# Attention products of 256 columns as three one-pass products, with split operands, rotary scores per pair of heads, and the first and last pair's steps moved

## The chip, the cores and the metric

The kernel runs on one core of a Trainium2 chip. The metric is the device time of one execution in microseconds. Three runs of the kernel before gave 2061.98, 2063.13 and 2064.1 us, a median of 2063.13 us.

## The reference

A decoder trunk of two layers over 256 positions, width 2048, all in float32. Layer A is chunked spatial gating (12 groups of 128 channels), layer B is multi-head latent attention (12 heads), and both stand beside a cross-attention of 4 heads of 128 channels into 256 memory tokens. After each follows a gated FFN of width 5632. What the change touches is the attention of layer B and the memory attention of both layers:

```
# MLA (layer B), per head h and block of 128 queries
q = (rmsnorm(q_lat, g_q_lat) @ w_uq).reshape(B, S, 12, 128 + 64)
q_nope, q_rope = q[..., :128], apply_rope(q[..., 128:], cos, sin)
s = (q_nope . (c_kv @ w_uk) + q_rope . k_rope) * 192 ** -0.5      # causal
o = softmax(s) @ (c_kv @ w_uv)

# memory attention, per layer, 4 heads of 128
s = einsum('bshd,bmhd->bhsm', q, k) * 128 ** -0.5
o = einsum('bhsm,bmhd->bshd', softmax(s), v)

x = x + concatenate([main, memory], -1) @ w_out
```

`rmsnorm`, the projections `w_in`, `w_kv_a`, `w_mem_kv`, the gMLP gate and the FFN are the rest, and the change leaves them alone but for the buffers that they pass through.

## The kernel before, in words

**Weights.** Every weight matrix is streamed in chunks of 128 x 1024 float32: SyncE (SP) starts the DMA into `raw` (4 buffers, line 100 on), ScalarE (ACT) rounds it to a `whi` tile of the one-pass type fp32r (L113, or L109 for the head-wise chunks of `w_uq`), and VectorE (DVE) writes the rest, raw minus whi, to `wlo` (L114, L110). `split_tile` (L94) gives both 5 buffers. A tile is written anew only when TensorE (PE) has read the chunk five earlier.

**Products.** Activations are held in the same form, a high half and a low half beside each other (`xhl`, `qhl`, `chl`, `mainhl`). A float32 product is then three one-pass products: whi x high (L152), whi x low (L153) and wlo x high (L155), 256 columns each. `gemm_tm` (L184 to L186) does the same with the activations as the stationary side and 512 columns.

**The heads' products** are different: their operands are plain float32 tiles, and PE works a float32 product itself, shown as two records each. These are, with `P` = 128: memory scores (L584, `kT` by `qm`, two products per head), memory output (L619, `mv` by `pT`, two per head), MLA scores without rotary part (L956, 128 columns for the first block of queries and 256 for the second), MLA rotary part (L957, `qr` by `krz`, the same sizes, each head by itself), and attention output (L990 with 256 columns, L991 with 128). PE also transposes the softmaxed scores (`turn` L981, `mturn` L608), and ACT copies the result from PSUM to `pT` (L983, L612).

**Layer B's loop** goes over the six pairs of heads, i = 0 to 5. One pass holds: `queries(i)` (two chunks of `w_uq`, ACT copies the result to `qn`), `rotary(i)` (`rotate` on GpSimd, POOL: L865, four L868, L869), `keys(i)` (one chunk of `w_uk`), for the pair before last the `turn`s and the memory `mturn`, for the last pair `scores` with softmax (DVE L963 to L974, ACT L969), then `attend` and `mout` for the pair before last, and `mscores(i-1)` (DVE L590 to L600, ACT L595). Ahead of the loop `values(0..2)` project `c_kv` through `w_uv` into `v`, which lies with the name `scratch` in the memory of the layer's first operand. Behind the loop stand `scores` of the last pair, and the last two pairs' `turn` and `attend` are hooks among the chunks of `w_out` (chunks 0, 1 and 3).

**Order.** The program is written once, and a scheduler decides, by its own estimate of times, in which order each engine gets its instructions; each engine then works its own list strictly in order, waiting on semaphores. So a written move shows as other neighbours in these lists.

Of the kernel before, what the change touches and what calls it, by code (L numbers as in the profile page):

```python
# [69 lines left out]
class Kernel:  # L70
# [359 lines left out]
    def start(self):  # L430
        nc, t, tc = self.nc, self.t, self.tc
        self.x = self.ap.tile([P, NB, S], F32, name="xT")
        self.xhl = self.ap.tile([P, NB, 512], F32R, tag="xhl", name=self.uid("xhl"))
# [5 lines left out]
        with tc.tile_pool(name="st", bufs=1) as st:  # L439
# [12 lines left out]
            def put_x(k, acc):  # L452
                for i in range(2):
                    self.split_gain(self.xhl[:, k + i, :], acc[:, i * S : (i + 1) * S], self.gain("g_mix", k + i))
                nc.scalar.activation(self.x[:, k : k + 2, :], acc.rearrange("p (k s) -> p k s", k=2), AF.Copy)
# [124 lines left out]
    def memory_scores(self, l, h, q, pool):  # L580
        nc = self.nc
        acc = self.psum()
        for sb in range(2):
            nc.tensor.matmul(  # L584
                acc[:, sb * S : (sb + 1) * S], q[:, sb * P : (sb + 1) * P], self.kT[l][:, h, :], start=True, stop=True
            )
        scale = 128 ** -0.5
        a3 = acc.rearrange("p (a m) -> p a m", a=2)
        mx = self.tmp(pool, [P, 2], "mx", 4)
# [3 lines left out]
        den = self.tmp(pool, [P, 2], "den", 4)  # L593
# [9 lines left out]
    def memory_turn(self, p, pool, bufs=2):  # L603
# [11 lines left out]
    def memory_out(self, l, h, pT, hl):  # L615
        nc, v = self.nc, self.mv[l]
        o = self.psum()
        for mb in range(2):
            nc.tensor.matmul(o[:, :S], v[:, mb, h * P : (h + 1) * P], pT[:, mb * S : (mb + 1) * S], start=mb == 0, stop=mb == 1)  # L619
        self.split(hl[:, GH + h, :], o[:, :S])  # L620
# [5 lines left out]

    def new_hl(self):
        self.xhl = self.ap.tile([P, NB, 512], F32R, tag="xhl", name=self.uid("xhl"))
        self.ssum = self.tmp(self.cp, [P, S], "ssum", 2)

    def next_operand(self, j, gain):
        x = self.x[:, j, :]
        if gain is None:
            self.split(self.xhl[:, j, :], x)
        else:
            self.split_gain(self.xhl[:, j, :], x, gain)
# [20 lines left out]
    def ffn(self, l, after=None, to_tokens=None, tokens=None):  # L657
# [5 lines left out]
        with self.tc.tile_pool(name=self.uid("ff"), bufs=1) as fp:  # L663
            g0 = 0
            for part, ng in enumerate(FF_GROUPS):
# [11 lines left out]
                for g in range(g0, g0 + ng):  # L677
# [14 lines left out]
                    self.gemm_fm(self.rows(up, g * 512, 512), ks, 4, lambda k: xhl[:, k, :], eg, hooks=first if g == 0 else {})  # L692
                    self.gemm_fm(self.rows(up, FF + g * 512, 512), ks, 4, lambda k: xhl[:, k, :], ev, hooks=turns)
# [21 lines left out]
    def layer_a(self):  # L715
        nc, t, tc = self.nc, self.t, self.tc
        w, xhl, rt, rb = t["w_in_a"][0], self.xhl, self.rt, self.rb
        x = lambda k: xhl[:, k, :]
        ks = list(range(NB))
        with ExitStack() as ctx:  # L720
# [5 lines left out]
            wT = la.tile([P, GH, P], F32, name="wT")  # L726
            bb = la.tile([P, GH, P], F32, name="bb")
# [52 lines left out]
            p = {}  # L780

            def scores(h):
                p[h] = self.memory_scores(0, h, qm[:, h, :], la)
# [4 lines left out]
            for c in range(3):  # L788
# [11 lines left out]
                if c < 2:  # L800
                    h = 2 * c
                    hooks = {
                        0: [lambda: gates(9)] if c == 0 else [],
                        2: [lambda h=h: scores(h)],
                        3: [lambda h=h: scores(h + 1)],
                        5: [lambda h=h: turn(h), lambda h=h: turn(h + 1)],
                        6: [lambda h=h: self.memory_out(0, h, p[h], hl)],
                        7: [lambda h=h: self.memory_out(0, h + 1, p[h + 1], hl)],
# [5 lines left out]
    def layer_b(self):  # L814
# [7 lines left out]
        x = lambda k: xhl[:, k, :]  # L822
        mm, tt = nc.tensor.matmul, nc.vector.tensor_tensor
        with tc.tile_pool(name="lb", bufs=1) as lb:
# [4 lines left out]
            krz = lb.tile([P, 2, S], F32, name="krz")  # L829
            nc.gpsimd.memset(krz, 0.0)  # L830
            qm = lb.tile([P, MH, S], F32, name="qm1")
            lt = ctx.enter_context(tc.tile_pool(name="lt", bufs=1))

# [28 lines left out]
            def rotate(dst, a):  # L862
# [6 lines left out]
                nc.gpsimd.tensor_tensor(dst, m, n, ALU.subtract)  # L869
# [14 lines left out]
            def rotate_key():  # L884
# [7 lines left out]
                for j in range(2):  # L892
                    r = slice(j * ROPE, (j + 1) * ROPE)
                    nc.gpsimd.tensor_tensor(krz[r, j, :], m[r, :], n[r, :], ALU.add)
# [8 lines left out]
            scratch = self.ap.tile([P, NB * 512], F32, tag="xhl", name="scratch")  # L903
            v = scratch[:, : 2 * GW].rearrange("p (a c) -> p a c", a=2)
            wuv = t["w_uv"][0].rearrange("r h v -> r (h v)")

            def values(c):
                def ev(tb, acc):
                    nc.scalar.activation(v[:, tb, c * 512 : (c + 1) * 512], acc, AF.Copy)
# [3 lines left out]
            for c in range(3):  # L913
                values(c)
            ctx.close()
            lp = ctx.enter_context(tc.tile_pool(name="lp", bufs=1))
# [6 lines left out]
            def queries(pr):  # L923
# [9 lines left out]
                qn[pr] = self.tmp(lp, [P, 3, S], "qn", 2)  # L933
# [3 lines left out]
            def keys(pr):  # L937
                kn[pr] = self.tmp(lp, [P, 2, S], "kn", 2)
# [6 lines left out]
            def rotary(pr):  # L945
                qr[pr] = self.tmp(lp, [P, S], "qr", 2)
                rotate(qr[pr], qn[pr][:, 2, :])

            def scores(h):
                pr, j = divmod(h, 2)  # L950
                sc = self.psum()
                for qb in range(2):
                    n = P * (qb + 1)
                    o = sc[:, qb * P : qb * P + n]
                    q = slice(qb * P, (qb + 1) * P)
                    mm(o, qn[pr][:, j, q], kn[pr][:, j, :n], start=True, stop=False)  # L956
                    mm(o, qr[pr][:, q], krz[:, j, :n], start=False, stop=True)  # L957
                mx = self.tmp(lp, [P, 2], "mx", 4)
                den = self.tmp(lp, [P, 2], "den", 4)
                p = self.tmp(lp, [P, 3 * P], "p", 3)  # L960
                part = (slice(0, P), slice(P, 3 * P))
                for qb in range(2):
                    nc.vector.tensor_tensor_reduce(  # L963
                        out=p[:, part[qb]], in0=sc[:, part[qb]], in1=self.mask[:, (1 - qb) * P :], scale=1.0, scalar=-3.0e38,
# [12 lines left out]
            def turn(h):  # L977
# [4 lines left out]
                pT = self.tmp(lp, [P, 512], "pT", 3)  # L982
                nc.scalar.activation(pT[:, : 3 * P], acc[:, : 3 * P], AF.Copy)  # L983
                pa[h] = pT

            def attend(h):
                pT = pa.pop(h)
# [149 lines left out]
```

## Time and profile before

| | |
|---|---|
| runs, median | 2063.13 us |
| profiled execution | 2063.35 us, of which span 2061.6 us (1.75 us lie around the span) |
| granted TensorE clock | 0.999 |
| PE | 2051.8 us busy, 16316 products |
| DVE | 1375.7 us busy (67%) |
| ACT | 1075.2 us busy (52%) |
| POOL | 141.0 us busy (7%) |
| HBM traffic | 387.88 MB read, 189 GB/s over the span |

A busy share is how much of the span an engine was inside some instruction. PE's records overlap, since products are pipelined, so a product's own duration (277 ns for 256 columns) is longer than the distance between two products; what a product costs the span is that distance, which the chain of the work that ended last gives.

### The profile page before, as it was taken

To read this page: it belongs to the slowest core of one execution; us is meant where nothing else is said; L and a number is where in the kernel's file an instruction comes from. 1 tells how busy PE (TensorE), PEld (TensorE's weight loads), DVE (VectorE), ACT (ScalarE), POOL (GpSimd) and SP (SyncE) were. 2 spreads that over 40 slices of the span, in tenths; PEclk is the share of its full clock that TensorE was granted. 3 is DMA by queue.
4 is the path that set the end of the run, shared out by engine and by line. 5 is a ranking of instruction groups with operands and counts; after the bars stand their busy time and mean duration, and the time that the engine had idled before them with its cause. 6 is when DMAs were issued, how large, how long until landed. Compare 5 with 4: busy or idle time off the path is not lost.

```text
span 2061.6 us, 39720 instructions
## 1 busy us (share of the span) xinstructions
PE 2051.8 (100%) x16316; PEld 1982.9 (96%) x16316; DVE 1375.7 (67%) x2051; ACT 1075.2 (52%) x1537; POOL 141.0 (7%) x200
## 2 busy tenths in 40 slices
PE   9999999999999999999999999999999999999998
PEld 8989999999999999999999999999988999889996
DVE  6656666777656767557788676776765677646765
ACT  7754644555434555345555574455543555435554
POOL 0000013100000000000042241400000000000000
PEclk9999999999999999999999999999999999999999
DMA  8665455666556665566655634565655666556653
GB/s 288 197 216 176 154 194 197 193 195 195 194 195 195 194 194 192 195 194 192 197 191 178 185 119 169 183 202 184 192 191 193 196 197 194 189 194 195 196 183 143
DMA packets 207690, 392.55 MB, mean 190 GB/s; under 512 B 14158, under 2 KB 23188, under 8 KB 207380
## 3 DMA queue, kind: packets, MB, share of 16 engines
q1 hardware_dynamic: 207316, 389.48, 58.5%
q8 instruction: 127, 2.08, 0.4%
q10 hardware_dynamic: 192, 0.54, 0.1%
q14 instruction: 55, 0.45, 0.1%
HBM read 387.88 MB, written 2.10 MB: 189 GB/s over the span
## 4 chain that ended last, share of the span: by engine, by line
PE 99%; ACT 0%; DMA 0%; DVE 0%; issue 0%; ACTq 0%
PE ps L152 26%; PE ps L153 26%; PE ps L155 26%; PE ps L185 6%; PE ps L184 6%; PE ps L186 6%; PE ps L507 1%; PE ps L956 0%; PE ps L957 0%; PE ps L400 0%; PE ps L619 0%; PE ps L584 0%; PE ps L767 0%; PE ps L990 0%; PE ps L981 0%; PE ps L608 0%
## 5 line engine op out<-in xcount | busy, mean ns | idle before, releaser
L114 DVE TENSOR_TENSOR wlo<-raw,whi 128x1024 fp32r<-128x1024 f32 x660 | 818.0, 1242 | 544.1 <-ACT whi L113 537.8
L113 ACT ACTIVATE whi<-raw 128x1024 fp32r<-128x1024 f32 x660 | 700.8, 1062 | 868.6 <-PE ps L153 661.9
L152 PE MATMUL ps<-xhl,whi 128*128 128x256 f32 x3264 | 764.6, 277 | 0.0
L153 PE MATMUL ps<-xhl,whi 128*128 128x256 f32 x3264 | 761.1, 276 | 0.0
L153 PEld LDWEIGHTS ps<-xhl,whi 128*128 128x128 f32 x3264 | 612.7, 188 | 0.5
L152 PEld LDWEIGHTS ps<-xhl,whi 128*128 128x128 f32 x3264 | 612.7, 188 | 0.5
L155 PE MATMUL ps<-xhl,wlo 128*128 128x256 f32 x3264 | 437.1, 276 | 0.0
L155 PEld LDWEIGHTS ps<-xhl,wlo 128*128 128x128 f32 x3264 | 400.6, 188 | 0.0
L152 PE MATMUL ps<-h,whi 128*128 128x256 f32 x704 | 163.6, 276 | 0.0
L153 PE MATMUL ps<-h,whi 128*128 128x256 f32 x704 | 163.6, 276 | 0.0
L185 PE MATMUL ps<-wlo,h 128*128 128x512 f32 x354 | 137.3, 388 | 0.0
L184 PE MATMUL ps<-whi,h 128*128 128x512 f32 x354 | 137.3, 388 | 0.0
L186 PE MATMUL ps<-whi,h 128*128 128x512 f32 x354 | 137.0, 388 | 0.0
L153 PEld LDWEIGHTS ps<-h,whi 128*128 128x128 f32 x704 | 131.9, 188 | 0.0
L152 PEld LDWEIGHTS ps<-h,whi 128*128 128x128 f32 x704 | 131.8, 188 | 0.0
L152 PE MATMUL ps<-mainhl,whi 128*128 128x256 f32 x512 | 119.7, 277 | 0.0
L153 PE MATMUL ps<-mainhl,whi 128*128 128x256 f32 x512 | 119.5, 276 | 0.0
L672 ACT ACTIVATE c<-a,cT 128x256 f32<-128x256 f32 x176 | 99.4, 588 | 0.0
L153 PEld LDWEIGHTS ps<-mainhl,whi 128*128 128x128 f32 x512 | 96.1, 188 | 0.0
L152 PEld LDWEIGHTS ps<-mainhl,whi 128*128 128x128 f32 x512 | 96.1, 188 | 0.0
L155 PE MATMUL ps<-h,wlo 128*128 128x256 f32 x704 | 94.1, 276 | 0.0
L232 DVE TENSOR_TENSOR a<-ps,rbc 128x256 f32<-128x256 f32 x176 | 69.9, 418 | 27.7 <-PE ps L155 27.7
(273 smaller groups left out, 2196.0 us busy)
## 6 DMA issues: line engine op xcount, KB each, us to landing
raw<-in_w_ffn_up SPq DMA_DIRECT2D x352, 512.0 KB, 3.5
raw<-in_w_ffn_down SPq DMA_DIRECT2D x176, 512.0 KB, 4.3
raw<-in_w_out SPq DMA_DIRECT2D x64, 512.0 KB, 4.4
raw<-in_w_in_a SPq DMA_DIRECT2D x56, 512.0 KB, 3.9
raw<-in_w_mem_kv SPq DMA_DIRECT2D x31, 512.0 KB, 4.6
raw<-in_w_in_b SPq DMA_DIRECT2D x16, 512.0 KB, 4.0
raw<-in_w_kv_a SPq DMA_DIRECT2D x9, 512.0 KB, 4.0
raw<-in_w_uq SPq DMA_DIRECT2D x12, 384.0 KB, 3.2
```

What stands on the lines that cost most here:

```text
L113: nc.scalar.activation(hi[:, :n], raw[:, :n], AF.Copy)
L114: nc.vector.tensor_tensor(lo[:, :n], raw[:, :n], hi[:, :n].bitcast(F32), ALU.subtract)
L152: mm(acc[:, :S], wh, x[:, :S], start=first, stop=False)
L153: mm(acc[:, :S], wh, x[:, S:], start=False, stop=False)
L155: mm(acc[:, :S], wl, x[:, :S], start=False, stop=last)
L184: mm(acc, xh, wh, start=first, stop=False)
L185: mm(acc, xh, wl, start=False, stop=False)
L186: mm(acc, xl, wh, start=False, stop=last)
L232: self.nc.vector.tensor_tensor(out, acc[:, :S], r, ALU.mult)
L507: nc.tensor.matmul(acc[:, :S], w[:, o : o + P], x, start=k == 0 and n == 0, stop=k == NB - 1 and n == 2)
L672: nc.scalar.activation(c, a, AF.Identity, scale=w(2), bias=w(3))
```

## The change

1. A helper `three` does a product as three one-pass products (high by high, high by low, low by high). Memory scores, memory output, the 256-column part of the attention output and the rotary part of the MLA scores use it. The rotary part is done once for both heads of a pair (256 columns for the first block of queries, 512 for the second), the scores of a pair come from two PSUM banks, one for each block of queries. The part `qn` by `kn` and the 128-column part of the attention output stay plain float32.
2. Their operands are split: `memory_split` per memory head (`kT`, `qm` with 256 columns each, `mv` with two of 128, on ACT and DVE each), the rotated queries (ACT and DVE), the rotary key once, the values at their eviction (DVE 128 x 512, three times), the turned scores `pT` and `mpT` (ACT high, DVE low).
3. Memory is found by: `whi` from 5 buffers to 4 (`wlo` keeps 5), the operand tile `xhl` as two half tiles, one of which holds `qn`, `kn` and the plain half of the values in layer B (`scratch`) and the other the split values and memory keys (`exact`), a shared slot in layer A, and fewer buffers for `pT` (3 to 2) and `mpT` (3 to 1).
4. Layer B's order: `queries(0)` and `rotary(0)` stand between `values(1)` and `values(2)`; `scores` of the last pair go into the first chunk's hook of `w_out`, and the later turns and attends to chunks 0, 2, 3 and 5.

```diff
     def split_tile(self, tag, moves=False):
-        w = self.wp.tile([P, 1088], F32R, tag=tag, name=self.uid(tag), bufs=5)
+        w = self.wp.tile([P, 1088], F32R, tag=tag, name=self.uid(tag), bufs=4 if tag == "whi" else 5)
...
+    def three(self, o, w, x, start, stop):
+        mm, (wh, wl), (xh, xl) = self.nc.tensor.matmul, w, x
+        mm(o, wh, xh, start=start, stop=False)
+        mm(o, wh, xl, start=False, stop=False)
+        mm(o, wl, xh, start=False, stop=stop)
+
+    def memory_split(self, l, h, q, keys, rest):
...
+        self.split(k, self.kT[l][:, h, :])
+        self.split(q2, q)
+        for tb in range(2):
+            c = slice(tb * P, (tb + 1) * P)
+            self.nc.scalar.activation(v2[:, c], v[:, tb, :], AF.Copy)
+            self.nc.vector.tensor_tensor(v2[:, S + tb * P : S + (tb + 1) * P], v[:, tb, :], v2[:, c].bitcast(F32), ALU.subtract)
...
-            nc.tensor.matmul(
-                acc[:, sb * S : (sb + 1) * S], q[:, sb * P : (sb + 1) * P], self.kT[l][:, h, :], start=True, stop=True
-            )
+            c, o = slice(sb * P, (sb + 1) * P), slice(S + sb * P, S + (sb + 1) * P)
+            self.three(acc[:, sb * S : (sb + 1) * S], (q[:, c], q[:, o]), (k[:, :S], k[:, S:]), True, True)
...
-        pT = self.tmp(pool, [P, 512], "pT", bufs)
-        nc.scalar.activation(pT, acc, AF.Copy)
+        pT = self.tmp(pool, [P, 1024], "mpT", bufs, F32R)
+        nc.scalar.activation(pT[:, :512], acc, AF.Copy)
+        nc.vector.tensor_tensor(pT[:, 512:], acc, pT[:, :512].bitcast(F32), ALU.subtract)
...
-            nc.tensor.matmul(o[:, :S], v[:, mb, h * P : (h + 1) * P], pT[:, mb * S : (mb + 1) * S], start=mb == 0, stop=mb == 1)
+            c, m = (slice(mb * P, (mb + 1) * P), slice(S + mb * P, S + (mb + 1) * P)), slice(mb * S, (mb + 1) * S)
+            self.three(o[:, :S], (v[:, c[0]], v[:, c[1]]), (pT[:, m], pT[:, 512:][:, m]), mb == 0, mb == 1)
...
-                nc.gpsimd.tensor_tensor(dst, m, n, ALU.subtract)
+                nc.gpsimd.tensor_tensor(m, m, n, ALU.subtract)
+                self.split(dst, m)
...
-                    o = sc[:, qb * P : qb * P + n]
-                    q = slice(qb * P, (qb + 1) * P)
-                    mm(o, qn[pr][:, j, q], kn[pr][:, j, :n], start=True, stop=False)
-                    mm(o, qr[pr][:, q], krz[:, j, :n], start=False, stop=True)
+                    q = [qr[pr][:, i * S + qb * P : i * S + (qb + 1) * P] for i in range(2)]
+                    both = bank[qb][:, : 2 * n].rearrange("p (j k) -> p j k", j=2)
+                    self.three(both, q, [k[:, :, :n] for k in krz], True, False)
+                    for j in range(2):
+                        mm(both[:, j, :], qn[pr][:, j, qb * P : (qb + 1) * P], kn[pr][:, j, :n], start=False, stop=j == 1)
...
-                mm(o[:, :S], v[:, 0, cols], pT[:, :S], start=True, stop=False)
-                mm(o[:, P:S], v[:, 1, cols], pT[:, S : S + P], start=False, stop=True)
+                self.three(o[:, :S], (vh[:, cols], vl[:, cols]), (pT[:, :S], pT[:, S:]), True, False)
+                mm(o[:, P:S], v1[:, cols], last, start=False, stop=True)
...
             for i in range(n):
-                queries(i)
-                rotary(i)
+                if 1 <= i <= MH:
+                    mparts(i - 1)
                 if i >= 1:
+                    queries(i)
+                    rotary(i)
                     keys(i)
...
-                    scores(2 * i - 2)
-                    scores(2 * i - 1)
+                    scores(i - 1)
...
-            scores(2 * n - 2)
-            scores(2 * n - 1)
...
-            hooks = {1: calls(attend, pairs[0]) + calls(turn, pairs[1]), 3: calls(attend, pairs[1])}
+            hooks = {
+                0: [lambda: scores(n - 1)] + calls(turn, pairs[0]),
+                2: calls(attend, pairs[0]),
+                3: calls(turn, pairs[1]),
+                5: calls(attend, pairs[1]),
+            }
```

What this makes of the engines' lists, at three places. First, PE in the loop's first pass that has all its parts (i = 2), behind the turns: before, in this order, the second half of the first head's scores, the second head's, both attends, the memory output and the memory scores (`kn`, `qn`: projected keys and queries; `krz`, `qr`: rotary ones).

```order
L956 MATMUL ps_14536<-kn_14334,qn_14321 128x256
L957 MATMUL ps_14536<-krz,qr_14325 128x256
L956 MATMUL ps_14552<-kn_14334,qn_14321 128x128
L957 MATMUL ps_14552<-krz,qr_14325 128x128
L956 MATMUL ps_14552<-kn_14334,qn_14321 128x256
L957 MATMUL ps_14552<-krz,qr_14325 128x256
L990 MATMUL ps_14568<-pT_14521,scratch 128x256
L991 MATMUL ps_14568<-pT_14521,scratch 128x128
L990 MATMUL ps_14573<-pT_14527,scratch 128x256
L991 MATMUL ps_14573<-pT_14527,scratch 128x128
L619 MATMUL ps_14578<-pT_14534,mv_85 128x256 x2
L584 MATMUL ps_14583<-kT_83,qm_13095 128x256 x2
```

And PE at the same place of the change, from the second block of queries on (L582 to L584 are the three products of `three`, `exact` holds the split values, `rest` the split memory queries and values, `scratch` the plain `qn` and `kn`):

```order
L582 MATMUL ps_14639<-krz_13160,qr_14408 128x512
L583 MATMUL ps_14639<-krz_13161,qr_14408 128x512
L584 MATMUL ps_14639<-krz_13160,qr_14408 128x512
L1001 MATMUL ps_14639<-scratch 128x256 x2
L582 MATMUL ps_14670<-pT_14616,exact 128x256
L582 MATMUL ps_14677<-pT_14625,exact 128x256
L583 MATMUL ps_14670<-pT_14616,exact 128x256
L584 MATMUL ps_14670<-pT_14616,exact 128x256
L582 MATMUL ps_14684<-mpT_14635,rest 128x256
L583 MATMUL ps_14677<-pT_14625,exact 128x256
L584 MATMUL ps_14677<-pT_14625,exact 128x256
L1040 MATMUL ps_14670<-pl_14617,scratch 128x128
```

Both heads' rotary products are now one, the attends are mixed with each other and with the first product of the memory output, and the first product that reads a low half of `pT` (L583) is the third of the attends.

Second, DVE at the same place of the program: before, what stands between the scaling of the memory scores (L600) and the maxima of the pair's scores (L963).

```order
L598 RECIPROCAL den_14408<-den_14408 128x2
L600 TENSOR_SCALAR mp_14407<-mp_14407,den_14408 128x256 x2
L110 TENSOR_TENSOR wlo_14783<-raw_14781,whi_14782 128x2x256
L110 TENSOR_TENSOR wlo_14783<-raw_14781,whi_14782 128x2x128
L110 TENSOR_TENSOR wlo_14809<-raw_14807,whi_14808 128x2x256
L110 TENSOR_TENSOR wlo_14809<-raw_14807,whi_14808 128x2x128
L963 ISA p_14543,mx_14541<-ps_14536,mask 128x128
```

And in the change (L617 scales the memory scores, L1011 takes the maxima):

```order
L615 RECIPROCAL md_14492<-md_14492 128x2
L617 TENSOR_SCALAR mp_14495<-mp_14495,md_14492 128x256 x2
L114 TENSOR_TENSOR wlo_14790<-raw_14788,whi_14789 128x1024
L110 TENSOR_TENSOR wlo_14930<-raw_14928,whi_14929 128x2x256
L110 TENSOR_TENSOR wlo_14930<-raw_14928,whi_14929 128x2x128
L241 TENSOR_TENSOR pT_14616<-ps_14612,pT_14616 128x256
L241 TENSOR_TENSOR pT_14625<-ps_14621,pT_14625 128x256
L1011 ISA p_14651,md_14650<-ps_14638,mask 128x128
L1011 ISA md_14650 128x1
L1011 ISA p_14661,md_14660<-ps_14638,mask 128x128
L1011 ISA md_14660 128x1
L630 TENSOR_TENSOR mpT_14635<-ps_14630,mpT_14635 128x512
```

The low halves of both heads' `pT` now stand on DVE behind two chunks' `wlo`, and that of `mpT` behind the first maxima.

Third, PE at the end of layer B: before, the last pair's scores and the first turns, ahead of the first product of `w_out` (`mainhl` by `whi`).

```order
L956 MATMUL ps_15145<-kn_15028,qn_15015 128x256
L957 MATMUL ps_15145<-krz,qr_15019 128x256
L981 MATMUL ps_15161<-ident,p_15089 128x128 x3
L981 MATMUL ps_15167<-ident,p_15105 128x128
L152 MATMUL ps_15173<-mainhl_14037,whi_15178 128x256
L153 MATMUL ps_15173<-mainhl_14037,whi_15178 128x256
```

And in the change, where they stand between two chunks of `w_out`:

```order
L155 MATMUL ps_15311<-mainhl_14108,wlo_15315 128x256 x2
L155 MATMUL ps_15312<-mainhl_14108,wlo_15315 128x256 x2
L582 MATMUL ps_15343<-krz_13160,qr_15183 128x256
L583 MATMUL ps_15343<-krz_13161,qr_15183 128x256
L584 MATMUL ps_15343<-krz_13160,qr_15183 128x256
L1001 MATMUL ps_15343<-scratch 128x128 x2
L582 MATMUL ps_15344<-krz_13160,qr_15183 128x512
L583 MATMUL ps_15344<-krz_13161,qr_15183 128x512
```

`w_out`'s first chunk now stands between the last pass of the loop and the last pair's scores.

More of the change, by code (lines that the diff above doesn't have):

```diff
@@ L633, in next_operand @@
         if gain is None:
-            self.split(self.xhl[:, j, :], x)
+            self.split(self.xhl[j], x)
         else:
-            self.split_gain(self.xhl[:, j, :], x, gain)
+            self.split_gain(self.xhl[j], x, gain)
         self.square_add(self.ssum, x, j == 0, self.cp)
```

122 lines of the change are left out of this document (76 added, 46 removed).

## The prediction

> **What bounds the kernel now.** I read the page's busy times and its chain first, then what PE waited for, to see whether any other engine has a part in the end.
>
> ```profile
> PE 2051.8 (100%) x16316; PEld 1982.9 (96%) x16316; DVE 1375.7 (67%) x2051; ACT 1075.2 (52%) x1537; POOL 141.0 (7%) x200
> ...
> PE 99%; ACT 0%; DMA 0%; DVE 0%; issue 0%; ACTq 0%
> ...
> L113 ACT ACTIVATE whi<-raw 128x1024 fp32r<-128x1024 f32 x660 | 700.8, 1062 | 868.6 <-PE ps L153 661.9
> ```
> ```profile
> PE ps L474 <- DVE ones L283: 1.1, 1, 1.1
> PE ps L325 <- DMA graw<-in_g_mem: 0.5, 1, 0.5
> ```
>
> PE fills 2051.8 of the span's 2061.6 us, the chain that ended last is PE for 99%, and PE's waits on others come to 1.6 us, both in the first microseconds. ACT in turn stands idle 661.9 us because PE has not yet released a `whi`. So the time is the sum of the distances between PE's products, and whatever the change takes off PE comes off the end, as long as the split operands are ready. Only those two things have to be priced.
>
> **What PE saves.** The distance between two products stands in the chain, since its pieces lie end to end. These are the chain's rows in the loop's second full pass of layer B, then in `values`, and in the FFN.
>
> ```profile
> 1193.20 0.22 PE ps L957 x2
> ...
> 1193.86 0.43 PE ps L957 x2
> 1194.29 0.43 PE ps L990 x2
> ...
> 1195.60 0.87 PE ps L619 x4
> 1196.46 0.86 PE ps L584 x4
> ...
> 1198.72 0.68 PE ps L155 x6
> ```
> ```profile
> 1159.85 0.23 PE ps L184
> ...
> 1166.42 0.23 PE ps L186
> ```
> ```profile
> 700.14 0.91 PE ps L155 x8
> ...
> 702.86 0.91 PE ps L155 x8
> ```
>
> A plain float32 product of 256 columns is two records and costs 0.432 us (0.43 for x2, 0.865 for x4), one of 128 columns 0.22. A one-pass product of 256 columns costs 0.68 / 6 = 0.1133 us. One of 512 columns costs (1166.42 - 1159.85) / 29 = 0.2266 us, since 30 products follow each other from the one row to the other. Three one-pass products of 256 columns are 0.34 us against 0.432. How many there are:
>
> ```profile
> L619 PE MATMUL ps<-pT,mv 128*128 128x256 f32 x32 | 8.2, 379 | 0.0
> L584 PE MATMUL ps<-kT,qm 128*128 128x256 f32 x32 | 8.2, 379 | 0.0
> ...
> L990 PE MATMUL ps<-pT,scratch 128*128 128x256 f32 x24 | 7.1, 380 | 0.0
> L957 PE MATMUL ps<-krz,qr 128*128 128x256 f32 x24 | 7.1, 379 | 0.0
> ...
> L957 PE MATMUL ps<-krz,qr 128*128 128x128 f32 x24 | 4.6, 275 | 0.0
> ```
>
> - Memory scores and outputs: 32 records each are 16 products each; 32 x 0.432 = 13.8 us go, 96 one-pass products (10.9 us) come: -2.9 us.
> - Attention output, 12 products: 5.2 us go, 36 x 0.1133 = 4.1 us come: -1.1 us.
> - Rotary scores: 12 x 0.432 + 12 x 0.22 = 7.8 us go. Per pair three products of 256 and three of 512 columns come, 18 x 0.1133 + 18 x 0.2266 = 6.1 us: -1.7 us.
>
> Together 26.8 us go and 21.1 us come, **-5.7 us**; of this 1.5 us lie in layer A, the rest in layer B. One more place is no term: `queries(0)` among `values` and the last pair's scores among `w_out` change places only, with the same products.
>
> That the new products go at 0.1133 us is read from L155, whose stationary block also changes with each product:
>
> ```profile
> L155 PEld LDWEIGHTS ps<-xhl,wlo 128*128 128x128 f32 x3264 | 400.6, 188 | 0.0
> ```
>
> A load takes 188 ns there, more than the distance of 113 ns, so loads are overlapped with products and with each other. The Trainium skill speaks against this: "TensorE: Matmul & The Clock Gate", section "The mechanism", says that a weight load overlaps running products only when its row group differs, and these loads all fill 128 rows. By that rule no product could follow the last by less than its load; this trace's 113 ns disagree with it, and I go by the trace (the rival for it is below).
>
> **What the splits cost.** They are ACT's and DVE's, and cost nothing while PE need not wait. In layer A and in `w_out` there is room. In layer B's loop I looked at DVE's load, pass by pass.
>
> ```profile
> 1190.41:1204.00 13.59, 13.59 (x105) 13.07 (x103) 9.65 (x29) 9.17 (x29) 5.48 (x8) 1.00 0.26 78
> 1204.00:1217.60 13.60, 13.60 (x105) 13.08 (x104) 9.84 (x28) 9.42 (x27) 5.14 (x7) 1.00 0.39 128
> 1217.60:1231.17 13.57, 13.57 (x104) 13.05 (x103) 9.43 (x27) 9.36 (x27) 5.43 (x6) 1.00 0.34 109
> ```
>
> After the length come PE, weight loads, DVE (9.4 to 9.8 us), ACT (9.2 to 9.4) and POOL (5.1 to 5.5). A pass of 13.59 us loses 0.28 us in the rotary scores, 0.18 in two attends, 0.37 in memory output and scores: 12.76 us. DVE gains per pass low halves of: rotated queries (256 columns), two `pT` (256), `mpT` (512), memory key and query (256 each), two value blocks (128). For prices:
>
> ```profile
> 1190.67 1.56 DVE L110 TENSOR_TENSOR wlo<-raw,whi 128x512 fp32r<-128x512 f32 x2 [0.60 <-ACT whi L109]
> ...
> 1197.46 0.74 DVE L241 TENSOR_TENSOR mainhl<-ps,mainhl 128x256 fp32r<-128x256 f32 x2
> ...
> 1202.27 1.02 DVE L110 TENSOR_TENSOR wlo<-raw,whi 128x512 fp32r<-128x512 f32 x2
> ```
>
> From SBUF, 768 columns in 1.02 us make 0.34 us per 256; from PSUM a low half of 256 is 0.37. So 0.34 + 2 x 0.37 + 0.7 + 2 x 0.34 + 0.5 = **2.9 us**, and DVE would be busy 12.3 to 12.8 of 12.76 us. No row shows a 128-column low half from SBUF; between nothing and a 256-column one (0.34) I take 0.25 each. ACT gains the same pieces less a cheaper copy, about 2 us, and stays at 11.5. So DVE goes from a spare 3.9 us per pass to about none, in the three passes that hold everything (i = 2 to 4). The last pass has no memory scores and splits, and the stretches ahead and behind are emptier.
>
> The wait this makes has a place. PE's first use of a low half is the third attend product, behind 2.33 us of scores and two attend products (0.23): 2.56 us after the memory turn's end. Before, these rows set it:
>
> ```profile
> 1188.51 0.62 DVE L600 TENSOR_SCALAR mp<-mp,den 128x256 f32<-128x256 f32 x2
> 1189.04 1.02 DVE L110 TENSOR_TENSOR wlo<-raw,whi 128x512 fp32r<-128x512 f32 x2
> ```
> ```profile
> 1191.50 0.39 PE L956 MATMUL ps<-kn,qn 128*128 128x128 f32 x2
> ```
>
> PE began the scores at 1191.50, so it would want the low half at 1194.06, about 0.4 us earlier with the first pass's savings ahead of it. DVE ended its `wlo` at 1192.23, after 0.60 us of waiting; now it has memory key, query and values (1.2 us), the rotated queries (0.34) and two halves of `pT` (0.74) to do in the same stretch: 1194.5 with that waiting kept, 1193.9 without. That is 0.2 to 0.8 us late; if those low halves run beside POOL at the price of 1190.67 (1.56 for 1.02, so +50% on 1.5 us), 0.8 us more. The other wait is the memory turn itself: the scaled `mp` was ready at 1189.13 and PE took it at 1191.07; with 1.5 us of new DVE work and about 1 us of high halves on ACT in front of it, it would be ready at 1191.6, 0.9 us behind a PE that comes 0.4 earlier; where half of that fills waits of before, it is early. What stands behind is the same list: PE holds back `attend`, `mout`, `mscores`, so the next maxima come as much later, and `wlo` are by then chunks ahead. I take 1.0 us for the first full pass, 0.3 for each of the two others, **+1.6 us**; ends 0 and 6 (each of three passes 2 us beyond its products).
>
> **`whi` with four buffers.** A chunk takes 702.86 - 700.14 = 2.72 us, of which the first 1.81 read `whi`; the copy takes 1.062 (L113). With five buffers a `whi` lies ready 5 x 2.72 - 1.81 - 1.06 = 10.7 us ahead of its use, with four 8.0. What delays ACT in the FFN and in `w_out` are evictions of a few us each, less than 8.0, so I take 0; the bound on the other side is where the lead fell lowest, and if that ran dry once per group of four blocks in the FFN, a few tenths each. Fewer buffers for `pT` and `mpT` only matter if PE is late anyway.
>
> **Sum.** 2063.35 (this execution: span 2061.6 and 1.75 around it) - 5.7 + 1.6 = 2059.2; the executed runs' median lies 0.2 below it, so **2059.0 us**.
>
> **Rivals.**
> - *All covers hold*: DVE's waits of before are just filled, no pass waits. 2063.1 - 5.7 = 2057.4. For it: PE mixes attend, output and scores so that low halves come last; against it the 12.8 of 12.76 us.
> - *DVE sets the pace of the loop.* Each of three passes ends 1 to 2 us behind its products, since the maxima, exponentials and scalings are a chain between DVE and ACT in which DVE also waits: +3 to +6, 2060.5 to 2063.5, mostly no change.
> - *DVE and POOL keep each other out* (slower). Rows beside POOL's rotation, whose four parts run together 4.43 us:
>
> ```profile
> 1173.56 1.03 DVE L110 TENSOR_TENSOR wlo<-raw,whi 128x512 fp32r<-128x512 f32 x2 [1.01 <-ACT whi L109]
> ...
> 1180.36 1.82 DVE L110 TENSOR_TENSOR wlo<-raw,whi 128x512 fp32r<-128x512 f32 x2 [0.99 <-ACT whi L109]
> ```
>
>  The same work takes 1.03 us without POOL and 1.82 with it. If all new low halves (2.9 us) fell beside POOL at 1.77 times their price, and POOL's longer time stretched `wlo` as well, a pass of DVE would be 9.7 + 5.1 + about 1.5 = 16.3 us, 3.5 over PE's; four such passes cost 14 us: 2071. It is slower than before from a pass of about 15.0 us on (12.76 + 9.0 / 4). Against it: POOL is busy 5.4 us of a pass and not all, and half of the new low halves read PSUM. The Trainium skill, "SBUF — State Buffer", section "Who interferes with whom", has the rule: a DVE operation with two SBUF inputs and a GpSimd operation that reads SBUF hold a shared port in turn, and the later one blocks fully. The rows agree with it as far as the 1.82 goes.
> - *The new products cost their loads*: 150 x 0.188 + 18 x 0.2266 = 32.3 us in place of 21.1 gives +5.5 and 2068.6. L155 speaks plainly against it.
>
> **How the numbers follow.** A difference of 0.2% (4.1 us, 2059.0 and 2067.3) is about what a measurement of this kernel can tell from none. Forecast, waits of 0.7 to 2.7 us (2058.1 to 2060.1): 0.45. All covers hold (2057.4, to 2058.1): 0.20. DVE sets the pace: 0.22. Ports: 0.08. Loads: 0.03. Something dearer that I don't see: 0.02. Faster by over 0.2%: the second and somewhat over half of the first, 0.45. Slower: 0.10 (the last three less a part of them that stays short). Within: 0.45. The range reaches from full cover at a slightly better price, 2056.8, to the upper end of a DVE-paced loop, 2064.0.
>
> **What would show it.** Right: PE's busy products less by 5.7 us of distance (memory scores at 0.34 x 2 per head in the chain), first waits of PE in the loop at the memory turn and the attends, for DVE's `mpT` and `pT` or ACT's, 1 to 3 us in all, DVE above 12 us per pass, none for `whi` in the FFN. Wrong: PE waits above 3 us in the loop (pace), passes longer than 13.59 us (ports), waits for L113 outside the loop (the fourth buffer), or three products in the chain that take more than 0.35 us (loads).

## The result, and the profile after

The changed kernel takes 2058.70 us, median of 16 runs (2057.99 to 2062.28), against 2063.12 us for the kernel before (16 runs, 2061.98 to 2064.22): a ratio of 0.998 with a 95% interval of 0.9972 to 0.9987. That is 0.2% faster: small, but clear of no change. The profiled execution's span is 2057.0 us, 4.6 less than before.

The page's busy times and chain, after:

```profile
PE 2046.9 (100%) x16348; PEld 1979.9 (96%) x16348; DVE 1396.0 (68%) x2113; ACT 1085.6 (53%) x1588; POOL 142.0 (7%) x200
...
PE 99%; ACT 0%; DVE 0%; DMA 0%; issue 0%; ACTq 0%
...
L113 ACT ACTIVATE whi<-raw 128x1024 fp32r<-128x1024 f32 x660 | 700.6, 1062 | 857.8 <-PE ps L153 632.3
```

PE is still the whole chain, with 32 records more and 4.9 us less of busy time. What PE waited for, after:

```profile
PE ps L474 <- DVE ones L283: 1.1, 1, 1.1
PE ps L583 <- DVE pT L241: 0.4, 1, 0.4
PE ps L325 <- DMA graw<-in_g_mem: 0.4, 1, 0.4
```

One wait is new, at the place that the prediction named: the first attend product that reads a low half of `pT`. The chain around it, in the loop's pass i = 2:

```profile
1189.92 0.53 ACT whi L109
1190.45 0.02 issue
1190.48 1.92 DVE wlo L110 x2
1192.39 0.34 DVE pT L241
1192.74 0.04 issue
1192.78 0.39 PE ps L583
1193.17 0.12 PE ps L584
```

The `wlo` pair took 1.92 us beside POOL's rotation (1.02 without it, as the prediction's rows show), and `pT` stood behind it. The wait row counts 0.4 us, from the end of PE's last record on; in the distance between the ends of two products it is 0.81 us in place of 0.12, so 0.69 us were lost, and 0.13 at the same product of the next pass. The two low halves of `pT` themselves, which read one input from PSUM, were not dearer beside POOL: 0.74 us, as in the run without the sine part (below), where POOL was idle then.

Since the first microseconds differ from one execution to the next (PE waits there for loads and their splits, 0 to 2 us at L507), the kernels are best compared by stretches. I took the ends of the same PE products in each trace and subtracted them. Layer A is counted from the end of the gate's projection to the first product of `w_out`; the entry is `values` with the first two passes' queries; a pass goes from the last `whi` product of one pass's queries to that of the next; the exit is from there to the 128th `whi` product of layer B's `w_out`. What lies between and behind these stretches (both FFNs, the rest of `w_out`, the end) agrees within 0.02 us for all kernels of the table.

| us | layer A | entry | i = 1 | i = 2 | i = 3 | i = 4 | exit | sum against before |
|---|---|---|---|---|---|---|---|---|
| before | 101.75 | 26.33 | 10.31 | 13.59 | 13.60 | 13.57 | 37.04 | |
| after | 100.55 | 26.37 | 9.85 | 13.52 | 12.97 | 12.87 | 35.75 | -4.3 |
| before, with the moves | 101.75 | 26.37 | 10.31 | 13.59 | 13.60 | 13.57 | 36.81 | -0.2 |
| after, without the moves | 100.55 | 26.33 | 11.34 | 14.33 | 12.85 | 12.87 | 37.54 | -0.4 |
| the same, plain scores first | 100.55 | 26.33 | 9.87 | 15.75 | 12.84 | 12.86 | 37.29 | -0.7 |
| after, turns early | 100.55 | 26.37 | 9.85 | 17.00 | 12.83 | 12.87 | 35.71 | -1.0 |
| after, no sine part | 100.55 | 26.37 | 9.85 | 12.85 | 12.85 | 12.87 | 35.75 | -5.1 |
| after, low halves twice | 100.55 | 26.37 | 9.85 | 14.17 | 13.06 | 12.99 | 36.01 | -3.2 |

So 4.3 us of the 4.6 come from the places of the change, and 0.3 from the start. The windows of three passes, from one pair's scores to the next, answer to those of before:

```profile
1190.35:1203.87 13.52, 13.11 (x109) 12.65 (x108) 12.72 (x39) 11.01 (x39) 5.58 (x7) 1.00 0.31 87
1203.87:1216.84 12.97, 12.97 (x109) 12.65 (x108) 11.68 (x36) 10.44 (x35) 5.57 (x8) 1.00 0.44 148
1216.84:1229.71 12.87, 12.87 (x109) 12.63 (x108) 10.23 (x32) 9.60 (x30) 5.41 (x7) 1.00 0.31 103
```

DVE (the number behind the weight loads) went from 9.7 to 12.7 us in the first and from 9.4 to 10.2 in the third; only in the first is PE less busy than the window is long.

### The profile page after: what moved, and what is told of

Same layout as the page of the kernel before. It is cut to its first block, busy times and chain, and to the rows that moved or that the text cites. A ratio compares the mean times of both kernels' runs of the same rounds, so it can differ in the third digit from the quotient of the medians.

```text
span 2057.0 us, 39914 instructions
## 1 busy us (share of the span) xinstructions
PE 2046.9 (100%) x16348; PEld 1979.9 (96%) x16348; DVE 1396.0 (68%) x2113; ACT 1085.6 (53%) x1588; POOL 142.0 (7%) x200
## 4 chain that ended last, share of the span: by engine, by line
PE 99%; ACT 0%; DVE 0%; DMA 0%; issue 0%; ACTq 0%
PE ps L152 26%; PE ps L153 26%; PE ps L155 26%; PE ps L185 6%; PE ps L184 6%; PE ps L186 6%; PE ps L507 1%; PE ps L400 0%; PE ps L583 0%; PE ps L584 0%; PE ps L582 0%; PE ps L1001 0%; PE ps L790 0%; PE ps L1115 0%; PE ps L1029 0%; DMA graw<-in_g_mem 0%
## 5 line engine op out<-in xcount | busy, mean ns | idle before, releaser
L113 ACT ACTIVATE whi<-raw 128x1024 fp32r<-128x1024 f32 x660 | 700.6, 1062 | 857.8 <-PE ps L153 632.3
```

What stands on the lines that cost most here:

```text
L113: nc.scalar.activation(hi[:, :n], raw[:, :n], AF.Copy)
```

## The experiments

My theory: the time is PE's distances, so the gain is the products', less the one wait at `pT`. The rivals: the fourth `whi` buffer, the moves as the true gain, DVE as the loop's pace.

**Four buffers for `whi`, nothing else.**

```diff
-        w = self.wp.tile([P, 1088], F32R, tag=tag, name=self.uid(tag), bufs=5)
+        w = self.wp.tile([P, 1088], F32R, tag=tag, name=self.uid(tag), bufs=4 if tag == "whi" else 5)
```

> The kernel before with one edit, four whi buffers. My theory (four are enough: a whi lies ready about 8.0 us ahead of its use in place of 10.7): no difference, span 2061.6 within 0.5 us, and no wait of TensorE on L113. The rival (the fourth-buffer ring runs dry in bursts of ScalarE): waits on L113 in the FFN or at the start, and 1 us or more on the span.

Measured: ratio 0.9998 (0.9989 to 1.0007), span 2061.0, and every stretch as long as before to 0.01 us. No wait of PE on L113. The buffer cost the kernel before nothing; that rival is out.

**The change without its moves.**

```diff
+            for c in range(3):
+                values(c)
-            for c in range(2):
-                values(c)
-            queries(0)
-            rotary(0)
-            values(2)
...
-                0: [lambda: scores(n - 1)] + calls(turn, pairs[0]),
...
+                1: calls(attend, pairs[0]) + calls(turn, pairs[1]),
```

> The changed kernel with the written order of before: queries(0) and rotary(0) inside the loop, the last pair's scores ahead of w_out, the hooks at chunks 1 and 3. My theory (the gain is the products' shorter distance, the moves only cover waits): the same TensorE distances, up to 1.5 us more in waits near the loop's entry and at the first turns, so span 2057.0 to 2058.5. The rival (the moves bring the gain): 2059.5 or more.

Measured: 2062.67 us, ratio 0.9999 (0.999 to 1.0008). The whole gain is gone, so my expectation of at most 1.5 us fell. The waits of PE:

```profile
PE ps L582 <- ACT qr L240: 2.5, 2, 1.3
...
PE ps L1026 <- DVE p L1019: 0.6, 1, 0.6
PE ps L583 <- DVE pT L241: 0.5, 1, 0.5
```

The first row is the rotated queries, at the first pair's scores and at the last pair's. POOL ends the first rotation 30.8 us behind the start of `values`, where it was 30.6 before; now ACT and DVE have to split it before PE can use it:

```profile
1179.26 0.72 POOL L901 TENSOR_TENSOR rm<-rm,rn 128x256 f32<-128x256 f32 x1
```
```profile
1180.49 0.39 PE L582 MATMUL ps<-krz,qr 128*128 128x256 f32 x1 [1.19 <-ACT qr L240]
```

By distances the waits are 1.47 (first scores), 0.75 (turn), 0.72 (`pT`), 1.53 (last scores) and 0.28 us (turn), 4.75 in all against 0.82 in the change: 3.9 us, which is what the stretches show (115.26 against 111.33 for layer B's). Both moves were taken back together; by the table 2.1 us lie at the first pair (entry to i = 4) and 1.8 at the last one (exit). (In the kernel before, and here, the first of the turns behind the loop stand ahead of `w_out` and the hooks in its chunks 1 and 3; the description of it names chunk 0 as well, which is wrong.)

**The moves alone, on the kernel before.** This tells whether the moves bring time themselves.

```diff
+            for c in range(2):
+                values(c)
+            queries(0)
+            rotary(0)
+            values(2)
...
+                0: calls(scores, pairs[1]) + calls(turn, pairs[0]),
```

> The kernel before with only the written moves of the change (queries(0) and rotary(0) between the values, the last pair's scores and the later turns and attends among w_out), all products plain, no splits. My present theory (a move brings nothing by itself, it covers waits that the splits make, and the kernel before has none): no difference, 2061.6 within 0.5 us on the span. The rival (the moves bring time in any kernel): 2 us less or more.

Measured: ratio 0.9999 (0.999 to 1.0008); the stretches change by -0.2 us. The moves bring next to nothing by themselves. They hide what the splits would cost.

**Plain scores first, without the moves.** In the change the rotary product opens the PSUM bank for both heads, so no other product of the pair can go before it.

```diff
-                    self.three(both, q, [k[:, :, :n] for k in krz], True, False)
                     for j in range(2):
-                        mm(both[:, j, :], qn[pr][:, j, qb * P : (qb + 1) * P], kn[pr][:, j, :n], start=False, stop=j == 1)
+                        mm(both[:, j, :], qn[pr][:, j, qb * P : (qb + 1) * P], kn[pr][:, j, :n], start=j == 0, stop=False)
+                    self.three(both, q, [k[:, :, :n] for k in krz], False, True)
```

> The run without the moves once more, with one edit: in the pair's scores the two plain products stand first in each bank and the three rotary ones behind them. There the waits for the rotated queries were 1.47 and 1.53 us (first and last pair), since the rotary product had to open the bank. My theory (the moves are worth so much because the rotary products come first and their operand is two engine steps later than before): with plain products to do first TensorE waits less for the rotated queries, about 0.5 us in place of 1.5 at the first pair and near 0 to 0.8 at the last, 1.5 to 2.5 us less than without the moves, so 2060.2 to 2061.2 on the runs. The rival (it is the splits' total load on VectorE and ScalarE, not the order in the bank): no change, 2062.5 or more.

Measured: 2062.65 us, no change on the runs. My number fell; it is the rival's, but not for its reason alone. The wait for the first rotated queries went (pass i = 1 from 11.34 to 9.87), and came back one pass later:

```profile
1190.17 0.61 PE L1026 MATMUL ps<-ident,p 128*128 128x128 f32 x3 [1.01 <-DVE p L1019]
1191.05 0.61 PE L1026 MATMUL ps<-ident,p 128*128 128x128 f32 x3 [0.27 <-DVE p L1019]
```

PE now waits at the turn for the softmax of the same scores (i = 2 from 14.33 to 15.75, both passes together 25.6 us as without the edit). Rotation, split, scores, softmax and turn are one chain, and a wait taken from one of its links goes to the next, unless the chain begins earlier. That is what the move of `queries(0)` does. The end of POOL's first rotation in the change, 9.7 us ahead of the row without the moves (0.5 of it is that execution's later start):

```profile
1169.51 0.74 POOL L901 TENSOR_TENSOR rm<-rm,rn 128x256 f32<-128x256 f32 x1
```

**No sine part on POOL.**

```diff
-                for i in range(4):
-                    q, o = (slice(k * HALF, (k + 1) * HALF) for k in (i, i ^ 1))
-                    nc.gpsimd.tensor_tensor(n[q, :], a[o, :], self.sinT[o, :], ALU.mult)
-                nc.gpsimd.tensor_tensor(m, m, n, ALU.subtract)
```

> The changed kernel without the sine part of the query rotation (four products and the subtraction on GpSimd are left out, so the rotated queries lack it). GpSimd's stretch per pass falls from 5.4 to about 1 us. My theory (the wait of 0.69 us at the first attend's low half comes from the wlo ahead of it on VectorE, which takes 1.92 us beside GpSimd in place of 1.02): wlo takes 1.0 to 1.1 there, and TensorE's wait at L583 falls below 0.15 us; span 2056.0 to 2056.5. The rival (VectorE simply has too much to do, or ScalarE brings the whi too late): the wait stays above 0.4 us.

Measured: the loop's stretches fall by 0.81 us and both waits are gone (i = 2 and 3 at 12.85); the span of 2057.3 (one execution) hides it, since the part up to the gate's projection took 1.05 us longer in it. DVE's rows:

```profile
1190.78 1.38 DVE L110 TENSOR_TENSOR wlo<-raw,whi 128x512 fp32r<-128x512 f32 x2
1192.09 0.41 DVE L241 TENSOR_TENSOR qr<-rm,qr 128x256 fp32r<-128x256 f32 x1
1192.43 0.74 DVE L241 TENSOR_TENSOR pT<-ps,pT 128x256 fp32r<-128x256 f32 x2
```

The `wlo` pair took 1.38 in place of 1.92 us, where I had expected 1.0 to 1.1. It also started earlier against PE (0.59 us ahead of the 512-column scores, where it was 0.16 behind), so two things worked against the wait, 0.54 and 0.75 us, while the rotated queries' low half (0.41 us) now stood between the pair and `pT`; the run doesn't say that the first alone would have done it. That POOL's work lies behind the wait is shown; that it is the shared port is not. The Trainium skill, "SBUF — State Buffer", "Who interferes with whom", would have the port's loser wait for a whole instruction; a stretch of 1.92 against 1.02 fits that, and so does a slower rate.

**The low halves of `pT` and of the rotated queries twice.**

```diff
                 self.split(dst, m)
+                tt(dst[:, S:], m, dst[:, :S].bitcast(F32), ALU.subtract)
...
                 self.split(pT, acc[:, :S])
+                tt(pT[:, S:], acc[:, :S], pT[:, :S].bitcast(F32), ALU.subtract)
```

> The changed kernel with the low halves of pT and of the rotated queries in layer B written twice: VectorE has 1.1 us more per pass. My theory (VectorE has almost no room in the first full passes, room later, and TensorE waits for what stands in its list ahead of the low half): the first full pass waits about 0.7 us more, the second 0.5 to 1.0 more, the later ones less; 1.2 to 2.5 us in all, span 2058.2 to 2059.5. The rival (VectorE sets the pace of the loop): 1.1 us more in each of five passes, 5 us, 2062. The other rival (VectorE has room): under 0.5 us.

Measured (one execution): 1.1 us more in the stretches, a little under what I had expected: 0.65 in i = 2, 0.1 in each of i = 3 and 4, 0.26 at the exit. DVE has no room in the first full pass and has it in the later ones. It does not set the pace of the loop, which would have been 5 us.

**Turns ahead of the keys.**

```diff
                     queries(i)
                     rotary(i)
-                    keys(i)
...
                 if i >= 1:
+                    keys(i)
                     scores(i - 1)
```

> The changed kernel with the turns written ahead of keys(i), so that the low halves of pT stand on VectorE ahead of the last wlo of the pass. My theory: the wait at L583 (0.8 us over two passes) goes, span 2056.0 to 2056.6. The rival (the wait moves to the turns, since the scaled scores are not ready 2.7 us earlier): a wait of TensorE at L1029 or L625 for VectorE, of 0.5 us or more in one or several passes, span 2057 to 2060.

Measured: 2061.73 us, and 3.3 us more than the change in the stretches; the rival was right.

```profile
PE ps L625 <- DVE mp L617: 1.2, 1, 1.2
...
PE ps L1029 <- DVE p L1022: 0.6, 2, 0.3
```

The first full pass takes 17.00 us, 4.2 more than the next one, which is as short as without any wait (12.83). By distances 2.5 us of that are waits, because neither the scores nor the memory scores are scaled yet. Another 1.6 are the products of `keys` behind them: the granted clock fell to 0.50 for 3.4 us there, and they follow at 0.213 us in place of 0.113 (the clock stands third from the end of the first row).

```profile
1188.95:1192.33 3.38, 3.38 (x18) 3.38 (x17) 1.89 (x3) 1.61 (x6) 2.39 (x3) 0.50 0.78 207
```
```profile
1189.63 0.42 PE L152 MATMUL ps<-chl,whi 128*128 128x256 f32 x1
1189.84 0.42 PE L153 MATMUL ps<-chl,whi 128*128 128x256 f32 x1
```

Not every execution of this kernel has that: the six whose mean clock was 0.998 took 2061.7 to 2063.1 us, the five with 0.999 took 2060.5 to 2060.9. So of the 3.3 us about half is the clock and not the rival's waits; with either half the run is slower than the change.

**A product left out, twice.** First the second of the three, then in another run the third.

```diff
         mm(o, wh, xh, start=start, stop=False)
-        mm(o, wh, xl, start=False, stop=False)
         mm(o, wl, xh, start=False, stop=stop)
```

> The changed kernel without the second of the three products (high by low is left out everywhere in the heads' products: 50 of 256 columns and 6 of 512). My theory (TensorE's distances are the time): 50 x 0.118 + 6 x 0.235 = 7.3 us less, and the wait for pT's low half goes as well, since nothing reads it: 2057.0 - 7.3 - 0.8 = 2048.9, up to 2050 if VectorE (11.7 to 12.7 us per pass) is then the longer one in the fullest passes. The rival (the heads' products lie beside something else that sets the pace): less than half of it, 2053.5 or more.

> The changed kernel without the third of the three products (low by high), where the run two_of_three left out the second. The operands stay split, and pT's low half is read. If the products' distances are the time, layer A loses 1.8 us as there, and the passes of the loop about 0.5 to 1 us each; if w_out then follows at 113 ns (65.3 us for the 128 blocks that took 69.1 there), the slower w_out was a state that PE had fallen into by the order of its list, and the span is 2051 to 2053. If w_out takes 69 us again, leaving products out itself makes it so, and the span is about 2056.

Measured (one execution each): span 2057.1 and 2051.8 us; my 2048.9 to 2050 for the first fell, the 2051 to 2053 for the second came. In layer A both give what the products cost, 1.8 and 1.7 us (16 products of 0.117). In layer B's stretches of the table 34 products of 256 and 6 of 512 columns (5.4 us) are gone, but the stretches fall by 2.6 and 3.1 us only: the passes i = 2 and 3 take 13.0 and 12.5, and 13.5 and 12.4 us, where 11.8 is what PE would need (12.85 without waits, less seven products of 0.118 and one of 0.235). So here PE begins to wait, in the second of the two for `pT` from DVE (0.51 and 0.24 us at L583), about a microsecond a pass below where the change stands; which chain sets that pace was not tested further. The first of the two lost 4.5 us elsewhere: its `w_out` of layer B and the FFN's first products, whose instructions are not touched, ran slower. The windows of 20 us in `w_out`, of that run, of the other one and of the change (the number of PE's products is in the brackets):

```profile
1260.00:1280.00 20.00, 20.00 (x169) 20.00 (x168) 12.06 (x13) 7.35 (x8) 3.04 (x5) 1.00 0.61 188
```
```profile
1260.00:1280.00 20.00, 20.00 (x179) 20.00 (x178) 13.34 (x15) 9.28 (x12) 4.41 (x6) 1.00 0.65 208
```
```profile
1260.00:1280.00 20.00, 20.00 (x179) 20.00 (x178) 13.82 (x16) 9.59 (x12) 5.98 (x7) 1.00 0.55 183
```

PE is full in all three and waits for nothing, at the same granted clock, and does 169 products in place of 179. I take it up in the last section.

**Other places of the operands.** The attends' products followed at 120 ns, not 113, and I had read their operands' places as the cause.

```diff
-        tiles = [self.ap.tile([P, NB // 2, 512], F32R, tag=f"xhl{i}", name=self.uid("xhl")) for i in range(2)]
+        tiles = [self.ap.tile([P, 4128], F32R, tag=f"xhl{i}", name=self.uid("xhl"))[:, :4096].rearrange("p (k c) -> p k c", k=NB // 2) for i in range(2)]
...
-            v1, (vh, vl) = plain[:, :GW], (exact[:, i * GW : (i + 1) * GW] for i in range(2))
+            v1, (vh, vl) = plain[:, :GW], (exact[:, 1043 + i * GW : 1043 + (i + 1) * GW] for i in range(2))
...
-                qr[pr] = self.tmp(lb, [P, 576], "qr", 2, F32R)[:, 19 : 19 + 512]
+                qr[pr] = self.tmp(lb, [P, 512], "qr", 2, F32R)
...
-                pT, last = self.tmp(lp, [P, 576], "pT", 2, F32R)[:, 13 : 13 + 512], self.tmp(lp, [P, P], "pl", 2)
+                pT, last = self.tmp(lp, [P, 512], "pT", 2, F32R), self.tmp(lp, [P, P], "pl", 2)
...
```

> The changed kernel with other places of the operands within their tiles: the split values 19 elements into their tile (they began at 0), pT at 0 (it began at 13), the rotated queries at 0 (19), the memory keys ahead of the values. My theory (the 7 ns by which the attends' products and the 9 ns by which the 512-column rotary ones follow each other later than elsewhere come from where the operands lie): attends 120 to 113 ns, rotary ones 236 to 227, 0.4 us less in all. The rival (they come from the change between plain and one-pass products or from other engines' traffic): the distances stay within 2 ns.

> Both the earlier turns and the other places of the operands. If both theories hold, 0.8 + 0.4 us less than the change: span 2055.6 to 2056.2. If neither, 2057 or more.

> As the run with other places of the operands, but each half of the operand tile is 4160 columns long in place of 4128, so that the second half begins a multiple of 256 bytes behind the first. My present theory (the 4896 products whose moving operand had shifted by 128 bytes against their weights followed at 120 ns in place of 113, and made the 35 us): these are back at 113.4 ns, the attends' products at 115 to 118, and the span is 2056.3 to 2057.0. The rival (the time came from the larger tiles or from the heads' operands): 2070 or more.

Measured: 2093.86 (one execution), with the earlier turns as well 2094.99 (ratio 1.0156, 1.0142 to 1.017) and, with a tile length of 4160 columns in place of 4128, 2058.68 us (0.9981, 0.9972 to 0.999). The first layout made the second half of the operand tile begin 128 bytes off, and the FFN's products on it slower. Its chain in the FFN, where the second half of the 16 blocks ends (0.99) and the first half of the next ones begins (0.91):

```profile
380.90 0.99 PE ps L155 x8
383.86 0.99 PE ps L155 x8
386.68 0.91 PE ps L155 x8
389.40 0.91 PE ps L155 x8
```

With a length of 4160 columns the distance is 256 bytes more and the FFN is back. The attends then follow at 118 ns in place of 120.7 without waits and the 512-column rotary products at 230 in place of 235, 0.2 us in all: the half of what I had expected, and below what the runs tell. No version here that does all the products beats the change.

## Why the prediction was right, point by point

- **What bounds it**: right. PE remains the chain, and what went from PE went from the end.
- **The products, -5.7 us**: the mechanism was right, the size 0.8 us too large. By the distances in the trace the heads' plain products took 26.87 us where they were replaced (predicted 26.8) and the new ones take 21.9 without their waits (predicted 21.1). The step that failed is "the new products go at 0.1133 us": they go at 115 to 121 ns (means by kind), and the 512-column ones at 232 to 236 in place of 227. The chain at the first pair's scores shows the two sizes (columns: start, length):

```profile
1178.82 0.11 PE ps L582
1178.93 0.11 PE ps L583
1179.04 0.12 PE ps L584
1179.16 0.44 PE ps L1001 x4
1179.60 0.23 PE ps L582
1179.83 0.24 PE ps L583
1180.07 0.24 PE ps L584
```

 The rival of exposed loads (188 ns each) did not come; no new product of 256 columns that waits for nothing stands at more than 127 ns. The three of an attend take 0.36 us, though, above the 0.35 that the prediction named as a sign of this rival: the sign was set too close. The Trainium skill's "TensorE: Matmul & The Clock Gate", "The mechanism", says that loads overlap with running products only when the row group differs, and these rows are against that too; the same section also lets a load into a background weight buffer go ahead, which they are not against.
- **The waits, +1.6 us**: 0.8 us too large, 0.69 in the first full pass and 0.13 in the second, at L583 and behind the `wlo` pair beside POOL, as the prediction had it (1.0 and 0.3). The memory turn, the other wait, did not come, nor did the third pass's; 0.8 us in all is below the 1 to 3 that were named as a sign of being right. DVE's 12.7 us in the first full pass is the figure predicted (12.3 to 12.8), in part by luck, since it includes the stretched `wlo` pair; the later ones held 11.7 and 10.2, because the memory head's low halves, priced in every pass, stand there less often (four in the first window, two in the second, none in the third).
- **`whi` with four buffers, 0**: right, and tried by itself on the kernel before.
- **The moves, "no term"**: right as a term against the kernel before, and tried by itself; but the prediction never said what they cover, and they cover 3.9 us, nearly all that the change wins. The working looked at the loop with the moves in it, found 1.6 us of waits and took the rest for granted.
- **The sum**: -4.1 predicted (-5.7 and +1.6) and -4.3 measured in the stretches, because two terms were each 0.8 us too large with opposite signs: -4.9 and +0.8. The remaining 0.2 us lie in the neighbouring one-pass products, those of `w_out` above all, which the sum did not have. The median of 2058.7 against 2059.0 is better than the working deserves, and luck.

## What to carry to other kernels

When a full engine gets cheaper work and its helpers get more, price the chain by which the helpers' results come back, from its first link: here rotation, split, scores, softmax and turn. A wait taken from one link shows up at the next, and here only an earlier beginning of the chain (the move) or less work in it (no sine part) removed it; so look at what is moved together with a change even if the move itself is free. Compare executions by stretches between the same instructions, since 0.8 us of a loop can be hidden by 1 us at the start.

## What the runs showed of the hardware that was not expected

The distance of one-pass products of 256 columns has two values, 113 and about 120 ns, at the same granted clock and with the same loads of 188 ns (medians). Which one holds depends on where the operands lie: with the second half of the operand tile 128 bytes further, 4896 products on it followed at 120.0 ns and the 4896 on the first half at 113.8 (means over the trace), about 30 us of that run's 35, and 128 bytes more brought 113.4 back. It does not depend on that alone: where the second product was left out, over 700 products in a row followed at 118 to 121 ns from 1251 us on, with every tile laid out as in the change, where they follow at 113.4. They came behind plain products (the last attend's, L1039) and got their distance back behind others (L265):

```profile
1336.58 0.96 PE ps L155 x8
1337.53 0.43 PE ps L265 x2
1339.79 0.91 PE ps L155 x8
```

What makes PE fall into the slower distance, and whether the same is behind the 115 to 121 ns of the new products, stays open; no run here separates the order of the products from their places.

The granted clock can halve behind waits far shorter than the 3.4 us for which it then stays down. In the run with the earlier turns, waits of 0.28, 0.27 and 1.19 us (PE's idle time) stood within 3.0 us ahead of it, and PE was busy for 1.7 of the last 3.4 us. Without the moves single waits of 1.19 and 1.26 us did not bring it down; PE was busy for 2.2 of the 3.4 us up to the end of each. The run with the earlier turns and the other places shows the fall too, at the same place of the program. The rule behind it was not tested.
